# RMSNorm with Swish on one core: the first store in two pieces, and the next load behind it

## The chip, the cores and the metric

The kernel runs on one core of one Trainium2 chip. The core has five engines that run side by side and meet through semaphores: TensorE (PE, without work here), VectorE (DVE), ScalarE (ACT), GpSimd (POOL) and SyncE (SP), which here only issues transfers. 16 DMA engines move the data between the chip's main memory (HBM) and the on-chip buffer (SBUF, 128 partitions). The metric is the device time of one execution in microseconds (us). Beside the plain runs there is one profiled execution, from which all durations come.

## The reference

```python
batch, seq, dim = 16, 1024, 512          # x: float32, gamma: 512 ones, eps: 1e-5
rms = np.sqrt(np.mean(x ** 2, axis=-1, keepdims=True) + eps)
x_norm = x / rms * gamma
return x_norm * (1.0 / (1.0 + np.exp(-x_norm)))
```

16,384 rows of 512 float32 numbers go in and as many come out: 33.55 MB each way, 67.1 MB in all.

## The kernel before

**Tiling.** The 16,384 rows are dealt to the 128 partitions, 128 rows to each. In this document a "row" of the plan is one row on every partition, 128 x 2 KB = 256 KB. The 128 rows of the plan lie in four groups (32, 48, 16, 32); within a group a partition's rows are neighbours in HBM, so that a transfer of n rows is 128 runs of n x 2 KB. The SBUF buffer `xb` is a ring of 96 rows; results are written in place. Rows 96 to 127 of the plan take the places of rows 0 to 31, so loads 96, 112 and 122 may be issued only when the rows 0 to 31 have been stored.

**Transfers.** All of them are issued by SP, in the order of a list that is written out by hand (`order`), into one hardware queue. `loads` and `stores` give first row and number of rows; a transfer is named by its first row here (load 80 is rows 80 to 95). Entries of the list are:

- `("load", a)`: issue the load (line 115).
- `("store", a)`: issue the store when ACT has finished all units of 8 rows that it covers (line 121; the wait is part of the instruction, on `s_swish`).
- `("landed", a)`: SP waits until load a has landed (line 166).
- `("stored", 0)`: SP waits until store 0 has landed. In the trace this wait stands at the load behind it (line 115).

At the end SP waits for all the other stores, which share one semaphore (line 170). The first nine loads (rows 0 to 79) go out in the first 6 us, with gamma between them. Around the change the list says: when load 64 has landed, store 0 (32 rows), and load 80 directly behind it; when store 0 has landed, loads 96, 112 and 122; when load 112 has landed, all the other stores, each as soon as its rows are computed.

**Computation.** It goes in 16 units of 8 rows. For each unit ACT squares and sums six rows (line 215) and DVE two (line 251; in the first unit they do four each), POOL adds eps and takes the power -1/2 (lines 183, 189), DVE multiplies by that and by gamma (line 260), and ACT applies Silu in place, one instruction for 8 rows (line 225, for the last two units line 245). ACT and DVE run this as loops; PE's queue waits for the loads and passes each unit on to ACT.

Of the kernel before, what the change touches and what calls it, by code (L numbers as in the profile page):

```python
# [9 lines left out]
def kernel(  # L10
# [7 lines left out]
    nc = tc.nc  # L18
# [10 lines left out]
    ring = 96  # L29
    loads = [(0, 4), (4, 4), (8, 8), (16, 8), (24, 8), (32, 16), (48, 16), (64, 11), (75, 5)]  # L30
    loads += [(80, 16), (96, 16), (112, 10), (122, 6)]
    stores = [(0, 32), (32, 32), (64, 16), (80, 16), (96, 24), (120, 8)]
    order = [("load", a) for a in (0, 4, 8)] + [("gamma", 0)]
    order += [("load", a) for a in (16, 24, 32, 48, 64, 75)]
    order += [("landed", 64), ("store", 0), ("load", 80)]
    order += [("stored", 0), ("load", 96), ("load", 112), ("load", 122)]
    order += [("landed", 112)] + [("store", a) for a in (32, 64, 80, 96, 120)]
    early = 2
    cn = 8
# [15 lines left out]
    store_at = {a: t for t, (a, _) in enumerate(stores)}  # L55
# [21 lines left out]
    junk_v = [sbuf(f"junk_v{j}", [P, D]) for j in range(own_first)]  # L77

    ld = [nc.alloc_semaphore(f"ld{t}") for t in range(len(loads))]
    st = [nc.alloc_semaphore(f"st{t}") for t in range(2)]  # L80
    s_gld = nc.alloc_semaphore("s_gld")
    s_zero = nc.alloc_semaphore("s_zero")
    s_half = nc.alloc_semaphore("s_half")
# [10 lines left out]
    def need(ins, sem, value):  # L94
        return ins.wait_op(sem, value, "sem-ge")
# [4 lines left out]
    def dram(ap, piece):  # L100
        a, n = piece
        g = max(g for g in range(len(groups)) if first[g] <= a)
        r = a - first[g]
        assert r + n <= groups[g], piece
        rows = ap[P * first[g] : P * (first[g] + groups[g])]
        return rows.rearrange("(p n) d -> p n d", n=groups[g])[:, r : r + n, :]

    def buf(piece):
        a, n = piece
        at = a % ring  # L110
        assert at + n <= ring, piece
        return xb[:, at : at + n, :]

    def load(t):
        return nc.sync.dma_start(
            out=buf(loads[t]), in_=dram(xf, loads[t])
        ).then_inc(ld[t], 16)

    def store(t):
        need(  # L120
            nc.sync.dma_start(out=dram(of, stores[t]), in_=buf(stores[t])),
            s_swish, ends[t],
        ).then_inc(st[min(t, 1)], 16)

    def check_order():
        issued, stored = [], set()
# [26 lines left out]
    for what, a in order[early:]:  # L153
        if what == "load":
            load(load_at[a])
        elif what == "store":
            store(store_at[a])
        elif what == "gamma":
            need(
                nc.sync.dma_start(  # L160
                    out=gamma4[0:P:32, :], in_=gamma.partition_broadcast(4)
                ),
                s_zero, 1,
            ).then_inc(s_gld, 16)
        elif what == "landed":
            nc.sync.wait_ge(ld[load_at[a]], 16)
        else:
            assert store_at[a] == 0
            nc.sync.wait_ge(st[0], 16)
    nc.sync.wait_ge(st[1], 16 * (len(stores) - 1))  # L170

    for k in range(1, K):
        for t, (a, n) in enumerate(loads):
# [152 lines left out]
```

## Time and profile before

| What | us |
|---|---|
| median of three runs | 159.87 |
| lowest and highest | 159.64, 160.97 |
| the profiled execution | 161.05 |
| its span, first to last instruction | 159.7 |
| store 0: issued, landed | 48.12, 70.94 |
| load 80: issued, landed | 48.51, 81.0 |
| loads 96, 112, 122: issued | 70.96 to 71.8 |
| store 32 and store 64: issued | 96.89, 97.27 |
| store 80, 96, 120: issued | 110.02, 131.31, 136.61 |

The page gives the busy time of each engine, the DMA engines' load in 40 equal slices of the span, and groups of instructions by line. A name such as `SPq L115` means SP's instruction queue at line 115 of the kernel. In a row of the timeline the first number is the start, the second the duration, and what stands in brackets is the idle time of the engine before it and what ended that. In a row of a waits view the numbers are the total, the count and the longest. In a row of a windows view they are the window, its length, the busy time of DVE, ACT and POOL with the number of instructions, the clock, the mean share of the 16 DMA engines that was busy, and GB/s; a DMA packet is put down to the window in which it starts, so in windows that are shorter than a packet (2.4 us for 64 KB) the share can be above 1 or far below it without a pause.

### The profile page before, as it was taken

What the parts mean: (1) busy time and instruction counts of PE and PEld (TensorE: products, weight loads), DVE (VectorE), ACT (ScalarE), POOL (GpSimd) and SP (SyncE); (2) the same over time, 40 slices, a digit from 0 to 9 for tenths busy, and PEclk for the clock granted to TensorE, in tenths of its full rate; (3) what the DMA queues carried; (4) which work ended last, traced back from release to release, by engine and by line L of the source; (5) the groups of instructions that cost most, each with busy time, mean ns of one, the idle gap of its engine ahead of it and who ended that gap; (6) DMA issues with size and microseconds to landing.
All of it is one profiled execution on the core that took longest, in us unless ns stands there. A gap on an engine that the chain in (4) does not pass through costs nothing. (4 is left out here: it accounts for less than half of the span.)

```text
span 159.7 us, 844 instructions
## 1 busy us (share of the span) xinstructions
DVE 107.7 (67%) x198; ACT 115.8 (72%) x205; POOL 42.9 (27%) x38
## 2 busy tenths in 40 slices
DVE  0151999798988989898906988989898992000000
ACT  3609389999999999999269999999999186200000
POOL 1040506062442606062403351606153300000000
DMA  7999999999899969969999999799699999999993
GB/s 267 451 412 447 415 505 394 394 525 394 384 421 509 525 263 525 525 254 402 501 410 394 447 404 579 318 476 525 279 493 402 402 460 451 488 431 406 394 390 148
DMA packets 2744, 67.12 MB, mean 420 GB/s; under 512 B 308, under 2 KB 308, under 8 KB 312
## 3 DMA queue, kind: packets, MB, share of 16 engines
q1 hardware_dynamic: 2744, 67.12, 98.1%
HBM read 33.56 MB, written 33.55 MB: 420 GB/s over the span
## 5 line engine op out<-in xcount | busy, mean ns | idle before, releaser
L260 DVE SCALAR_TENSOR_TENSOR xb<-xb,rstd,gamma_sb 128x512 f32 (+1 forms) x128 | 86.1, 747 | 0.0
L215 ACT ACTIVATE junk<-xb 128x512 f32 (+1 forms) x94 | 54.6, 580 | 13.3 <-ACTq L98 11.7
L225 ACT ACTIVATE xb<-xb x14 | 50.4, 3603 | 0.7 <-ACTq L98 0.7
L251 DVE SCALAR_TENSOR_TENSOR junk_v<-xb 128x512 f32 (+1 forms) x34 | 22.1, 690 | 23.0 <-DVEq L98 23.0
L189 POOL TENSOR_TENSOR rstd<-aeps,neg_half 128x8 f32<-128x8 f32 x16 | 31.7, 1984 | 1.3
L183 POOL TENSOR_SCALAR aeps<-ms 128x8 f32<-128x8 f32 x16 | 10.3, 647 | 79.3 <-DVE junk_v L251 79.3
L215 ACT ACTIVATION_READ_ACCUMULATOR junk<-xb 128x1 f32 x94 | 17.7, 188 | 0.0
L245 ACT ACTIVATE xb<-xb 128x4096 f32<-128x4096 f32 x2 | 7.2, 3616 | 5.0 <-DVE xb L260 5.0
L251 DVE DVE_READ_ACCUMULATOR junk_v<-xb 128x1 f32 x34 | 2.8, 83 | 0.0
L227 ACT ACT_TABLE_LOAD x1 | 1.3, 1283 | 1.9 <-PEq L62 1.9
L269 DVE LOAD_MASK_SELECT gamma_sb<-gamma x1 | 0.0, 14 | 2.2 <-DMA gamma<-in_gamma_dram 2.2
L178 POOL MEMSET gamma<- 128x512 f32 x1 | 0.5, 525 | 1.5 <-POOLq L62 1.5
L269 DVE STREAM_SHUFFLE gamma_sb<-gamma 128x512 f32<-128x512 f32 x1 | 0.7, 719 | 0.0
L307 POOL MEMSET const-float32-0.0<- 128x1 f32 x1 | 0.1, 98 | 0.2 <-issue 0.2
L179 POOL MEMSET neg_half<- 128x8 f32 x1 | 0.1, 105 | 0.0
L307 POOL MEMSET const-uint8-127<- 128x1 uint8 x1 | 0.1, 102 | 0.0
L307 POOL MEMSET const-bfloat16-1.0<- 128x1 bf16 x1 | 0.1, 101 | 0.0
L307 POOL MEMSET const-float32-1.0<- 128x1 f32 x1 | 0.1, 98 | 0.0
## 6 DMA issues: line engine op xcount, KB each, us to landing
xb<-in_x_dram SPq DMA_DIRECT2D x4, 4096.0 KB, 30.0
out_dram<-xb SPq DMA_DIRECT2D x2, 4096.0 KB, 31.8
xb<-in_x_dram SPq DMA_DIRECT2D x3, 2048.0 KB, 13.8
out_dram<-xb SPq DMA_DIRECT2D x1, 6144.0 KB, 23.5
xb<-in_x_dram SPq DMA_DIRECT2D x1, 2816.0 KB, 43.0
xb<-in_x_dram SPq DMA_DIRECT2D x1, 2560.0 KB, 25.5
xb<-in_x_dram SPq DMA_DIRECT2D x2, 1024.0 KB, 5.7
out_dram<-xb SPq DMA_DIRECT2D x1, 2048.0 KB, 23.0
```

The lines of the kernel that those rows point to most:

```text
L178: nc.gpsimd.memset(gamma4, 0.0).then_inc(s_zero, 1)
L179: nc.gpsimd.memset(neg_half, -0.5).then_inc(s_half, 1)
L183: nc.gpsimd.tensor_scalar(out=aeps[k % 2], in0=ms[min(k, 1)], scalar1=eps_f, scalar2=None, op0=ALU.add,),
L189: nc.gpsimd.tensor_tensor(out=rstd[:, k * cn : (k + 1) * cn], in0=aeps[k % 2], in1=neg_half, op=ALU.pow),
L215: nc.scalar.activation(out=dummies[j], in_=rows[j], func=AF.Square, scale=inv_d**0.5, accum_out=sums[:, j : j + 1],)
L225: nc.scalar.activation(out=rows, in_=rows, func=AF.Silu).then_inc(s_swish, 1)
L227: nc.scalar.preload_act_table_set("silu_and_others")
L245: nc.scalar.activation(out=rows, in_=rows, func=AF.Silu), s_norm, n + 1
L251: ins = nc.vector.scalar_tensor_tensor(out=junk_v[j], in0=rows[j], scalar=inv_d, in1=rows[j], op0=ALU.mult, op1=ALU.mult, accum_out=to[:, ...
L260: ins = nc.vector.scalar_tensor_tensor(out=rows[j], in0=rows[j], scalar=factors[j], in1=gamma_sb, op0=ALU.mult, op1=ALU.mult,)
L269: need(nc.vector.stream_shuffle(gamma_sb, gamma4, [0] * 32), s_gld, 16).then_inc(s_gamma, 1)
L307: nc = _bacc.Bacc("TRN2", target_bir_lowering=False, num_devices=1)
```

## The change

Store 0 is cut into a store of 30 rows and one of 2, issued one behind the other. Load 80 is no longer issued together with the store: SP first waits until the 30 rows have landed, then issues load 80. Then it waits until the 2 rows have landed and issues loads 96, 112 and 122. Each of the two stores has a semaphore of its own; the other stores share the third.

```diff
-    stores = [(0, 32), (32, 32), (64, 16), (80, 16), (96, 24), (120, 8)]
+    stores = [(0, 30), (30, 2), (32, 32), (64, 16), (80, 16), (96, 24), (120, 8)]
...
-    order += [("landed", 64), ("store", 0), ("load", 80)]
-    order += [("stored", 0), ("load", 96), ("load", 112), ("load", 122)]
+    order += [("landed", 64), ("store", 0), ("store", 30)]
+    order += [("stored", 0), ("load", 80), ("stored", 30), ("load", 96), ("load", 112), ("load", 122)]
...
-    st = [nc.alloc_semaphore(f"st{t}") for t in range(2)]
+    st = [nc.alloc_semaphore(f"st{t}") for t in range(3)]
...
-        ).then_inc(st[min(t, 1)], 16)
+        ).then_inc(st[min(t, 2)], 16)
...
         else:
-            assert store_at[a] == 0
-            nc.sync.wait_ge(st[0], 16)
-    nc.sync.wait_ge(st[1], 16 * (len(stores) - 1))
+            nc.sync.wait_ge(st[store_at[a]], 16)
+    nc.sync.wait_ge(st[2], 16 * (len(stores) - 2))
```

Both stores wait for the same number of finished units (four), since row 30 and row 31 belong to the fourth unit. What is computed, and the bytes that are moved, stay the same.

## The prediction

> **What bounds the kernel now.** I read the page first, its busy shares and its row of the DMA engines:
>
> ```profile
> span 159.7 us, 844 instructions
> DVE 107.7 (67%) x198; ACT 115.8 (72%) x205; POOL 42.9 (27%) x38
> ...
> DMA  7999999999899969969999999799699999999993
> ...
> q1 hardware_dynamic: 2744, 67.12, 98.1%
> ```
>
> No compute engine is busy for three quarters of the span; the 16 DMA engines are, for 98.1% of it. A microsecond in which they idle is therefore a microsecond of kernel time, and everything else is cover. (A packet counts in the slice where it starts, so a 6 is no hole: in the trace's own table of packets no engine rests over 31 ns between two packets, from its first to its last.) The second view is busy time by windows, at the start, in the steady part and at the end; the last columns are DMA share and GB/s:
>
> ```profile
> 0.00:1.00 1.00, 0.00 (x0) 0.00 (x0) 0.19 (x4) 1.00 0.00 0
> 1.00:2.00 1.00, 0.00 (x0) 0.08 (x1) 0.09 (x1) 1.00 0.88 197
> 2.00:3.00 1.00, 0.00 (x0) 1.00 (x1) 0.48 (x2) 1.00 1.00 426
> ...
> 4.00:48.00 44.00, 32.89 (x66) 35.20 (x72) 14.39 (x12) 1.00 1.01 431
> ...
> 157.00:158.00 1.00, 0.00 (x0) 0.00 (x0) 0.00 (x0) 1.00 0.08 33
> 158.00:159.00 1.00, 0.00 (x0) 0.00 (x0) 0.00 (x0) 1.00 0.08 33
> ```
>
> Three things matter here. An issue into an empty queue moves nothing for 1 us. The steady rate is 431 GB/s: one row of the plan (128 x 2 KB = 262,144 B) takes 0.608 us. And after 157 us about one DMA engine of 16 still works: one engine is late, and it alone sets the last 1.5 us. The third view is SyncE's (SP's) timeline around the change, then what the waits of SP and ACT were worth:
>
> ```profile
> 48.12 0.35 SPq L121 DMA_DIRECT2D out_dram<-xb  x1
> 48.51 0.43 SPq L115 DMA_DIRECT2D xb<-in_x_dram  x1
> ```
> ```profile
> 70.96 1.29 SPq L115 DMA_DIRECT2D xb<-in_x_dram  x3
> ```
> ```profile
> SPq L115 <- DMA out_dram<-xb: 22.0, 1, 22.0
> ```
> ```profile
> 81.16 0.60 ACT L215 ACTIVATE junk<-xb 128x512 f32 x1 [4.33 <-ACTq L98]
> ```
>
> SP issues store 0 at 48.12 and load 80 right behind it, waits 22.0 us for store 0 to land, and issues loads 96, 112 and 122 at 70.96. All that time load 80 lies in the queue, so no DMA engine runs out. Issue-to-landing times of single transfers, from the same trace: store 0 22.8 us (landed 70.94), load 80 32.5 us (landed 81.0), load 0 at time zero 4.70 us.
>
> **The change, part by part.**
>
> *The split.* Same bytes, one more DMA. SP pays one more issue at 48.5, 0.33 to 0.43 us by the rows above; it is hidden by load 75, which is in the queue until it lands at 51.1 (issued 5.53, landing 45.6 us later). Per engine 8 packets of 64 KB (2.42 us each) become 8 of 60 KB and 8 of 4 KB. 8 KB packets take 0.309 us where the 64 KB rate gives 0.303, so eight more packets cost about 8 x 0.007 = 0.05 us; and this falls in a stretch that ends with a wait anyway. I take 0.
>
> *The moved load 80.* Its issue goes from 48.51 to the landing of the 30 rows. What is then queued is only the 2-row store, 2 x 0.608 = 1.21 us. Against it stands the loop "last byte moved, landing seen, next DMA issued, stream at full rate". The trace has one transfer into an empty queue: load 0, 4 rows, 4.70 us from issue to landing, of which 4 x 0.608 = 2.43 us is data. The rest, 2.27 us, holds the same pieces: issue and start 1.4 to 1.8 us (by packets, engine by engine), landing 0.45 us behind the last packet. Landing to SP's next issue: 0.02 us (70.94 to 70.96). The hole is 2.27 + 0.02 - 1.21 = 1.08 us on the engine that lands last.
>
> *What goes with it.* Today's turn from store to load isn't free either. Load 80 lands 10.06 us after store 0, its 16 rows are worth 9.73: 0.33 us. The packet table shows where: all 16 engines' last packets of store 0 are stretched, by 0.06 to 0.63 us, while load 80 stands behind them. In a hole of 1.08 us this turn is swallowed: 1.08 - 0.33 = 0.75 us. Bounds: with 0.45 us of landing, the 1.01 us to the first packet and nothing for a slow first packet, 0.45 + 0.02 + 1.01 - 1.21 = 0.27 us, less the turn about 0; with the longest landing of store 0 (0.67 us), the slowest start (1.77 us) and no turn saved, 0.67 + 0.02 + 1.77 - 1.21 = 1.25 us. I take **0.7 us**, near the full sum, since load 0 is the only row of a start on an empty queue.
>
> *The two waits.* Behind the first on SP stand load 80, the second wait, loads 96, 112, 122 and all later stores. The 2 rows land some 1.2 us behind the 30; the three loads then go out at about 70.5 to 71, as today (70.96), with 9.7 us of load 80 before them: cost 0. ACT feels load 80: today it idles 4.33 us until 81.16 for it, and would idle 0.7 us more, with VectorE and GpSimd behind it. That is hidden at the end: the 24-row store is issued at 131.31 when its Silu is done, while the store before it lands at 140.3 at last and at 138.0 on the first engine, 6.7 us ahead; it needs 2.27. Queue and computation shift together, so this cover of over 4 us stays. Without it the 0.7 us would not count twice either, as both are late by the same amount.
>
> **The sum.** The profiled execution took 161.05 us, 159.7 of span and 1.35 around it; plus 0.7 is a span of 160.4 and 161.75 us. That execution stands 1.2 us above the median of the runs, 159.87 (159.64 to 160.97); its late engine may be that difference. The step is the same for both: **160.6 us**.
>
> **The Trainium skill, two rules.** Both are in its page "DMA: Bandwidth & Descriptors", section "Latency and other measured facts". It gives about 0.6 us to the first byte for a DMA issued by SyncE or ScalarE. By it the loop would be an estimated 0.45 + 0.02 + 0.6 = 1.07 us, below the 1.21 us of the two rows, and there would be no hole. The trace disagrees: the first packet starts 1.01 us after issue, at time zero. It also gives 0.2 us for an access to HBM, and 2 us under high load, which it calls the main part of a DMA's fixed cost; by that, with 2 us of landing for 0.45, the estimated hole is 2.3 us after the turn. The store's 0.67 us under full load speaks against it.
>
> **The rivals.**
>
> *Covered.* A warm queue starts at once, the two rows last as long as the loop, and the bound of about 0 above holds: 159.9. For it: time zero is a cold start, its first packets took 0.4 to 0.8 us over their 0.309. Against: nothing in this trace shows a start that is shorter. The rule on the first byte would give this. Chance 0.17.
>
> *Slower by the late engine.* Today one engine loses 0.63 us in its last packet of store 0 and 0.51 in its first of load 80, 1.13 in all, and another 1.19 at the turn from load 122 to store 32 (98.3 to 100.3). If that is what a turn costs a weak engine, and the median run is free of it, a queue that starts anew into draining writes could bring it out each time, on top of the hole: 0.7 + 1.13 = 1.8, 161.7 us. It decides from 0.9 us of extra lateness on the engine that lands last. Against: the hole lets the writes drain first. Chance 0.15.
>
> *Slower by a long landing.* The 30 rows' completion takes 2 us instead of 0.45, as the rule on HBM under load has it: 0.7 + 1.5 = 2.2, 162.1 us. All store landings in the trace are 0.33 to 0.67 us behind the last packet. Chance 0.05.
>
> *The late engine set right.* Its 1.13 us at the turn vanish in the hole, and with separate turns the second lateness too: 0.7 - 1.13 - 1.19 = -1.6, 158.3 us. Both have to go. Chance 0.05.
>
> That the change doesn't do what it says I give nothing: in the compiled order load 80 stands behind both stores and waits for the first's semaphore, load 96 for the second's.
>
> **How the numbers follow.** The forecast, a hole of 0.2 to 1.25 us after the turn and so 160.0 to 161.2, has 0.58. With covered (from 159.5, where the runs' own spread lies) and the late engine (to 161.9) it makes 0.90: range 159.5 to 161.9. One per cent, 1.6 us, is about what a measurement of this kernel can tell from no change, as its three runs lie 1.33 us apart. Slower by more: the two slow rivals and a little of the forecast's upper end, 0.22. Faster by more: most of the last rival, 0.04. The rest, 0.74, is within 1%.
>
> **What would show it.** On SP: two stores at 48.1 and 48.5, one load at 69.2 to 69.7, three at 70.5 to 71. In the window 69 to 72 a real hole in the DMA's packets, about 1 us on each engine, that is not there today; load 80 landing at 81.2 to 81.8 and ACT's wait before unit 10 growing by the same amount; the rest of the run shifted by that, with no second hole. The start term is wrong if load 80's first packet comes less than 1 us, or over 1.8 us, after its issue. The landing term is wrong if SP issues load 80 after 70.2. The forecast is wrong as a whole if the hole is there and the end doesn't move, which would put the late engine, not the queue, in charge of the time.

## The result, and the profile after

The changed kernel takes 161.11 us in the median (161.03 to 161.39, six runs), the kernel before 159.80 (159.64 to 160.97, six runs beside them): a ratio of 1.006, with a 95% interval of 1.0031 to 1.009. In a second set of runs the same two gave 161.51 and 159.68, ratio 1.0098 (1.008 to 1.0116). So the change costs 0.6 to 1.0%, between 1.0 and 1.6 us by the ratios; the medians themselves lie 1.3 and 1.8 us apart. The forecast was 160.6 us, 0.7 over before, in a range of 159.5 to 161.9: right in sign and range, and low by 0.3 to 0.9 us in the cost (by the medians, 0.6 to 1.1).

The page of the kernel after, in the same rows:

```profile
span 159.8 us, 845 instructions
...
DVE 107.7 (67%) x198; ACT 115.7 (72%) x205; POOL 42.8 (27%) x38
...
DMA  7999999999999996979999999979969999999996
```

The span is 159.8 against 159.7 us, which seems to say that nothing happened. The reason is the profiled execution of the kernel before, which had the late DMA engine; a second profile of it, below, has a span of 158.1. In the mean of the 16 engines the last store landed 1.5 us later, at 159.20 us against 157.72. Busy times are unchanged, as they have to be. SP's timeline of the kernel after shows the new order, and behind it the time from issue to landing of load 80 alone (the transfer issued at 69.32):

```profile
48.12 0.82 SPq L121 DMA_DIRECT2D out_dram<-xb  x2
69.32 2.61 SPq L115 DMA_DIRECT2D xb<-in_x_dram  x4
```
```profile
DMA to landing us min/median/max: 12.3/12.3/12.3
```

Load 80 goes out at 69.32, when the 30 rows have landed, and lands at 81.6. Its 16 rows are 9.73 us of data, so some 2.5 us are fixed. The windows view around this issue:

```profile
68.50:70.05 1.55, 1.55 (x3) 1.55 (x3) 1.55 (x1) 1.00 0.79 322
70.05:70.41 0.36, 0.36 (x2) 0.36 (x3) 0.36 (x1) 1.00 0.00 0
70.41:70.95 0.54, 0.54 (x2) 0.54 (x3) 0.00 (x1) 1.00 3.28 971
```

In the middle window no packet starts, and by the trace's packet table none is running: the last packet of the two rows ends at 70.05, the first of load 80 starts at 70.42, 1.10 us after its issue. Engine by engine the pause is 0.38 to 1.35 us; from 66 to 74 us the engines idle 0.79 us each in the mean, where those of the kernel before idle nowhere. The rest is as it was: loads 96, 112 and 122 go out from 70.55 on, and no other pause follows. ACT's wait for load 80 has grown by 0.6 us:

```profile
81.75 0.60 ACT L214 ACTIVATE junk<-xb 128x512 f32 x1 [4.96 <-ACTq L98]
```

### The profile page after: what moved, and what is told of

Same layout as the page of the kernel before. It is cut to its first block, busy times and chain, and to the rows that moved or that the text cites. A ratio compares the mean times of both kernels' runs of the same rounds, so it can differ in the third digit from the quotient of the medians.

```text
span 159.8 us, 845 instructions
## 1 busy us (share of the span) xinstructions
DVE 107.7 (67%) x198; ACT 115.7 (72%) x205; POOL 42.8 (27%) x38
```

## The experiments

The theory is the hole: SP waits for a landing before it issues, and while landing, issue and start take their time, only the rows queued behind the awaited store keep the DMA engines busy. Rivals: the split costs by itself; any start of loads behind drained stores costs the same, however long the pause; the late engine decides. "Stretch" below is worked out from the packet table: what packets take beyond the median packet of their size, summed over a window and divided by 16 engines. "The turn" is the passage of the full queue from one direction to the other, from stores to loads or back.

### The split alone

```diff
-    order += [("landed", 64), ("store", 0), ("store", 30)]
-    order += [("stored", 0), ("load", 80), ("stored", 30), ("load", 96), ("load", 112), ("load", 122)]
+    order += [("landed", 64), ("store", 0), ("store", 30), ("load", 80)]
+    order += [("stored", 0), ("stored", 30), ("load", 96), ("load", 112), ("load", 122)]
```

> The first store stays in two pieces of 30 and 2 rows, but load 80 is issued together with them again, so the queue never runs short. Hole theory (the cost is the time in which the queue is empty): as before, 159.8 us, within 0.2. Split theory (the two pieces cost by themselves): about 161, as the changed kernel. The profile should show no pause of the DMA engines near 70 us.

Measured: 160.43 us against 159.97 before, ratio 1.0019 (1.0 to 1.0037). No engine pauses from 66 to 74 us. The split is thus not the main cost, though it is over the 0.2 us that were expected at most: 0.3 us by the ratio, 0.46 by the medians. The stretch from 66 to 73 us, the turn from store to load, is about 0.6 us an engine here (0.56 or 0.65, by the median 4 KB packet of this kernel or of the changed one), and 0.27 in the kernel before (0.19 in its second profile). All of it lies in the 4 KB packets ahead of the turn; load 80's packets take their median. In the changed kernel it is the other way round: the 4 KB packets take their median, and the stretch of 0.58 us lies in load 80's packets. So the split's dear turn is no part of what the changed kernel loses.

### The wait alone

```diff
-    order += [("landed", 64), ("store", 0), ("load", 80)]
-    order += [("stored", 0), ("load", 96), ("load", 112), ("load", 122)]
+    order += [("landed", 64), ("store", 0)]
+    order += [("stored", 0), ("load", 80), ("load", 96), ("load", 112), ("load", 122)]
```

> The first store is whole again (32 rows), but load 80 waits for its landing, so that nothing is queued behind the store. Hole theory: 2.27 us from the fixed part of load 0's landing, plus 0.02, less the turn of 0.33 us that goes with it: 2.0 us over before, 161.8; with the 0.4 us by which the changed kernel exceeded its forecast, 162.2. Turn theory (what costs is that loads start anew behind drained stores, however long the pause): as the changed kernel, 161.1.

Measured: 162.32 us against 159.97, ratio 1.0139 (1.0116 to 1.0163), 2.2 us. Idle 2.07 us an engine. The windows view of this kernel, from the end of its store on:

```profile
69.50:71.50 2.00, 2.00 (x4) 2.00 (x7) 1.15 (x1) 1.00 0.00 0
71.50:73.50 2.00, 1.60 (x3) 2.00 (x9) 0.00 (x0) 1.00 0.96 279
```

For 2 us no packet starts. The store's last packets end between 69.67 and 70.15, SP issues load 80 at 70.62, and its first packet starts at 71.58. This is the wait's price without cover, and it falls with the hole theory, not with the theory that the price doesn't depend on the pause.

### The cover, row by row

The second store with 1, 3, 4 and 8 rows in place of 2; the first has the rest of 32. The edit for 4 rows, the others likewise:

```diff
-    stores = [(0, 30), (30, 2), (32, 32), (64, 16), (80, 16), (96, 24), (120, 8)]
+    stores = [(0, 28), (28, 4), (32, 32), (64, 16), (80, 16), (96, 24), (120, 8)]
...
-    order += [("landed", 64), ("store", 0), ("store", 30)]
-    order += [("stored", 0), ("load", 80), ("stored", 30), ("load", 96), ("load", 112), ("load", 122)]
+    order += [("landed", 64), ("store", 0), ("store", 28)]
+    order += [("stored", 0), ("load", 80), ("stored", 28), ("load", 96), ("load", 112), ("load", 122)]
```

> Pieces of 31 and 1 rows, load 80 issued when the 31 have landed. 1 row covers 0.61 us. Hole theory: half way between whole store (2.2 us over before) and 2 rows (1.0 to 1.6), so 1.6 to 1.9 over before, 161.4 to 161.7 us. A theory of thresholds: 161.1, as with 2 rows.

> Pieces of 29 and 3 rows, load 80 issued when the 29 have landed. 3 rows cover 1.82 us. Hole theory: between 2 rows (1.0 to 1.6 us over before) and 4 rows (0.1): one row less of cover is 0.61 us, so 0.4 to 0.9 over before, 160.2 to 160.6 us. A theory of thresholds (any drained write costs the same) would put it at 161.1 or at 159.8.

> Pieces of 28 and 4 rows, load 80 issued when the 28 have landed. Hole theory: 4 rows are 2.43 us of cover, the loop takes 2.29, so the hole is closed: 159.8 us, at most 0.3 over before. Turn theory: the same 161.1 as with 2 rows.

> Pieces of 24 and 8 rows, load 80 issued when the 24 have landed. Hole theory: 8 rows are 4.86 us of cover, no hole: 159.8 us, as before. Turn theory: 161.1. If it is clearly below before, a late issue of load 80 has a gain of its own, up to the 0.33 us of the turn.

| Rows queued behind | Median, before beside it | Ratio (95%) | Idle an engine, 66 to 74 us | Stretch an engine, 66 to 73 us |
|---|---|---|---|---|
| 0 | 162.32, 159.97 | 1.0139 (1.0116 to 1.0163) | 2.07 | 0.64 |
| 1 | 161.61, 159.88 | 1.0102 (1.0073 to 1.013) | 1.11 | 0.72 |
| 2 | 161.11, 159.80 | 1.006 (1.0031 to 1.009) | 0.79 | 0.58 |
| 2, again | 161.51, 159.68 | 1.0098 (1.008 to 1.0116) | 0.82 | 0.66 |
| 3 | 160.47, 159.88 | 1.0048 (1.0028 to 1.0068) | 0.17 | 0.68 |
| 4 | 160.20, 159.97 | 1.0007 (0.9989 to 1.0026) | 0 | 0.58 |
| 8 | 160.14, 159.97 | 1.0006 (0.9981 to 1.0032) | 0 | 0.22 |

The price falls with each row; with four and with eight rows it can't be told from nothing. The stretch does not follow the rows: from 0 to 4 rows it is 0.58 to 0.72 us and lies in load 80's packets, also where no engine pauses; only with 8 rows is it as in the kernel before (0.27 and 0.19), and lies in the store's last packets again. Load 80's time from issue to landing, with 0, 1 and 3 rows behind the store, one row from each kernel's answer in this order:

```profile
DMA to landing us min/median/max: 12.4/12.4/12.4
```
```profile
DMA to landing us min/median/max: 12.2/12.2/12.2
```
```profile
DMA to landing us min/median/max: 12.5/12.5/12.5
```

Less 9.73 us of data this is a fixed part of 2.5 to 2.8 us, where load 0 at time zero has 2.27. With 2.7 us in place of 2.27, chosen afterwards from these, and a turn of 0.25 us that is paid anyway, a hole of 2.7 - 0.608 n - 0.25 gives 2.4, 1.8, 1.2, 0.6 and 0 us for 0 to 4 rows. The packet table needs no such choice: idle time and stretch, less the 0.23 us of stretch before (mean of two profiles), are 2.5, 1.6, 1.1 and 1.2, 0.6, 0.3 and for 8 rows 0. Measured, by the ratios: 2.2, 1.6, 1.0 to 1.6, 0.8, 0.1 and for 8 rows 0.1. None of these versions is faster than the kernel before; 4 or 8 rows only bring it back.

### Both kernels again, for a second trace

> The kernel before once more, for a second trace. If one DMA engine's lateness is chance, the span comes out near 158.4 us instead of 159.7, with the engines' last packets less than 1.5 us apart, and the time near 159.8. If it belongs to the kernel, one engine is again about 1.5 us behind the rest after 157 us.

> The changed kernel once more. Besides its time (161.1 us), its trace answers whether the second loss comes again: the first profile had packets of load 122 stretched at 98 to 100 us, 0.4 us an engine against 0.1 in the kernel before. Theory H (the hole only, and the stretch is chance): the stretch is absent or of another size, the time stays at 161.1. Theory H+T (the pause leads to a costlier turn at load 122): 0.3 to 0.5 us again.

The second profile of the kernel before, its page's first row and one window at the end, and then the kernel after in the same stretch:

```profile
span 158.1 us, 844 instructions
...
157.00:158.00 1.00, 0.00 (x0) 0.00 (x0) 0.00 (x0) 1.00 0.01 0
```
```profile
157.00:158.00 1.00, 0.00 (x0) 0.00 (x0) 0.00 (x0) 1.00 0.99 426
158.00:159.00 1.00, 0.00 (x0) 0.00 (x0) 0.00 (x0) 1.00 0.69 295
```

The late engine is gone: from 157 us on, when the first profile of the same program had one engine at work (share 0.08 in each of two windows), nothing is left. That execution took 159.43 us. So not every execution of the kernel before has a late engine, and the two first profiles could not be compared at their ends. In this pair the 16 engines of the kernel after are at work for another 1.7 us in the mean, so the time is lost by all, not by one.

Where it is lost, by landings (last engine) in this second pair: load 80 lands at 81.64 against 80.12, 1.5 us later; load 96 at 91.32 against 89.83, 1.5; load 122 at 102.19 against 99.87, 2.3. A second loss of some 0.4 us or more thus seems to come at load 122. The stretch from 97 to 103 us shows it as well: 0.44 and 0.50 us an engine in the two profiles of the kernel after, 0.09 and 0.15 in those before. It was expected to vanish if it were chance; it came again.

### The second loss

```diff
-    order += [("landed", 112)] + [("store", a) for a in (32, 64, 80, 96, 120)]
+    order += [("landed", 96)] + [("store", a) for a in (32, 64, 80, 96, 120)]
```

> The changed kernel, with the later stores released by the landing of load 96 instead of load 112, so that store 32 is issued some 6 us earlier, near 91.3 us, with 16 rows in the queue before it instead of 6. If the stretched packets at 98 to 100 us come from the issue itself, they move to 91 to 94 us; if they come from the turn from loads to stores, they stay at 98 to 100 us, and the time stays at 161.1; if they come from a queue that is nearly short there, they vanish and the time falls by 0.3 to 0.4 us.

> The same edit on the kernel before: store 32 issued near 90.7 us. If the turn at 98 to 100 us costs it its late engine because the store comes late, the time falls by up to 0.3 us and its spread (159.64 to 160.97) narrows; otherwise 159.8, as before.

On the changed kernel: 161.36 us, ratio to the kernel before 1.01 (1.0082 to 1.0118); store 32 is issued at 91.19, and the stretch from 96 to 106 us is 0.85 us, at the old place. So neither the issue itself nor a queue that is nearly short makes it; it goes with the turn from loads to stores. On the kernel before: 159.86 us, 1.0019 (0.9996 to 1.0041), and the spread didn't narrow (159.53 to 161.46).

Then the two last loads as one, so that the turn is made by 32 KB packets:

```diff
-    loads += [(80, 16), (96, 16), (112, 10), (122, 6)]
+    loads += [(80, 16), (96, 16), (112, 16)]
...
-    order += [("stored", 0), ("load", 80), ("stored", 30), ("load", 96), ("load", 112), ("load", 122)]
-    order += [("landed", 112)] + [("store", a) for a in (32, 64, 80, 96, 120)]
+    order += [("stored", 0), ("load", 80), ("stored", 30), ("load", 96), ("load", 112)]
+    order += [("landed", 96)] + [("store", a) for a in (32, 64, 80, 96, 120)]
```

> The changed kernel with loads 112 and 122 joined into one load of 16 rows, and the later stores released by the landing of load 96, so that the turn from loads to stores at 98 to 100 us is made by packets of 32 KB in place of 12 KB. If the stretch of 0.4 to 0.5 us an engine is a matter of the small packets at that turn, it goes, and the time is 160.7 to 160.9 us; if every such turn behind a pause is stretched, it stays, near 161.3.

> The same edit on the kernel before, as the partner of the run above. The hole alone should then be their difference: 1.1 to 1.3 us (1.08 reckoned from load 0, less the turn of 0.2 to 0.3, plus first packets that are slower). 159.4 to 159.8 us, without a clear difference from the kernel before.

Changed kernel: 161.62 us, 1.0098 (1.0073 to 1.0123), stretch from 96 to 106 us 0.97 us. Kernel before: 160.28 us, 1.0031 (1.0003 to 1.0058), stretch 0.93, so the expectation of "no difference" was missed for this one. Between the two medians lie 1.3 us, between the ratios 1.1; 1.1 to 1.3 were expected of the hole.

The small packets are not the cause: with larger ones the stretch doesn't fall. But the early store alone raises it, in both kernels alike: 0.85 and 0.84 us with store 32 issued early, 0.97 and 0.93 with the two last loads joined as well, where the changed kernel had 0.44 and 0.50 and the kernel before 0.09 and 0.15. (The turn of the kernel before begins at 96.4 us in these two versions, so a window from 97 us on misses a third of its stretch.) So with the early store the changed kernel has no more of it than its partner, and the extra 0.35 us are seen only with the store in its old place.

What a stretch here costs in time isn't shown: with 0.4 us more of it the changed kernel with the early store took 161.36 us, between its two medians of 161.11 and 161.51. And the partners' profiles in these last two pairs, 161.46 and 161.29 us, had a late engine and lie 1.6 and 1.0 us above the medians of their kernels, so they can't fix what the turn costs there. Nor does the stretch simply follow the pause: with 0 to 8 rows of cover it was 0.30, 0.51, 0.44 to 0.50, 0.04, 0.24 and 0.04. Why the turn is dearer in the changed kernel stays open.

## Why the prediction was right, and where it was off

**The bound.** Right. The DMA engines are full; the versions that made them pause became slower, the more the longer the pause, and those without a pause stayed within 0.5 us of the kernel before.

**The split, taken as 0.** With load 80 issued early it measured 1.0019, 0.3 us with an interval from 0 to 0.6. My argument, 8 more packets at 7 ns, looked at the packets' own time and not at the turn behind them, which went from 0.19 and 0.27 us to about 0.6. For the changed kernel the 0 was right all the same: its 4 KB packets, with nothing queued behind them, take their median.

**The hole.** The mechanism is shown: the pause is in the packets, its size falls with each row of cover, and it closes at 4 rows, where 2.43 us of cover outlast landing, issue and the first packet's start. What doesn't close there is the slow start: 0.58 us of stretch in load 80's packets, gone with 8 rows. To this extent the rival holds by which any start behind drained stores costs the same. The times of these two versions (1.0007 and 1.0006) don't tell them apart. The dates were right: load 80 issued at 69.32 (69.2 to 69.7 forecast), the first of the three loads at 70.55 (about 70.5 to 71), the first packet 1.10 us after its issue (1 to 1.8), load 80 landed at 81.59 (81.2 to 81.8).

**The size.** This is the step that was off, mostly by one term, the loop: 2.27 us taken from load 0 at time zero; 2.5 to 2.8 measured. With the changed kernel's own 2.54 us the sum is 2.54 + 0.02 - 1.21 = 1.35 us in place of 1.08, and the packets say the same: 0.79 us idle and 0.58 us of stretch in load 80's packets. I had asked whether a warm queue would start faster than the cold one; it starts no faster (0.96 to 1.10 us to the first packet against 1.01), and 15 of the 16 engines' first packets of load 80 are stretched by 0.3 to 1.1 us against their median, as at time zero. The idle time alone is three times the 0.27 us of my lower bound, since SP waits for the slowest of 16 engines and the engines start one after the other: their last packets of the 30 rows end between 68.34 and 68.79 us, and their first ones of load 80 start between 70.42 and 70.94. The second term is the turn that the hole swallows. It is saved, as forecast, since no store packet is stretched any more; but 0.33 us was the figure of one landing, on the engine that came last, and in the mean of the engines the turn is 0.27 us in that profile and 0.19 in the second. Both terms together make 1.1 to 1.3 us (0.79 + 0.58 - 0.27, and 0.82 + 0.66 - 0.19 in the second pair), where I had 0.75. My upper bound of 1.25 us was nearly the value, but by another sum, with no turn saved.

**No second loss.** "The rest shifted, with no second hole" holds for pauses. But there were 0.35 us more of stretched packets at the turn from loads to stores, which no step of mine had. With them the sum is 1.4 to 1.7 us, against 1.0 to 1.6 by the ratios and 1.3 and 1.8 by the medians. That they add to the time is argued, not shown: with 1 row of cover, where the turn from loads to stores is as dear (0.51 us), pause and slow start alone already make up the measured 1.6 us.

**The two waits and ACT.** Right: the three loads cost nothing, since load 80 lay in the queue. ACT waited longer for load 80, 4.96 us for 4.33, and 5.09 for 3.55 in the second pair, and the end didn't feel it: the 24-row store went out at 131.9 us, while the store before it landed at 139.6 on its first engine, 7.7 us ahead.

**The rivals.** "Covered" fell: the shortest start into an empty queue was 0.96 us (with the wait alone), so the Trainium skill's 0.6 us to the first byte ("DMA: Bandwidth & Descriptors", section "Latency and other measured facts") doesn't hold here as the time from SP's issue to a packet's start. Counted from the end of SP's issuing instruction, which itself takes 0.33 to 0.39 us, the first packet comes after 0.62 to 0.76 us, near that figure. The long landing fell too: the 30 rows landed 0.51 us behind their last packet, not 2 us, with all engines still at work. The late engine fell as a cause: it came in three of four profiles with load 80 behind an undivided store (before, not before again, and the two variants of before) and in neither of the kernel after. I had named it as what may set the profiled execution 1.2 us above the median; the second profile, 159.43 us without it, bears that out. The other side of that rival, the late engine set right, has something for it: the six first runs of the kernel after lie within 0.4 us of each other, those of the kernel before within 1.3. But in the second set both spread alike (0.8 and 0.9 us), and no run of the changed kernel was faster than the median before.

## What to carry to other kernels

Where the DMA queue is the bound and an issue waits for a landing, price the cover: issue to landing less the data's own time (here 2.5 to 2.8 us) must be covered by what is queued behind the awaited transfer; here 4 rows of 256 KB, about 1 MB, were enough for no pause and no measurable cost, and each row short of it cost about 0.6 us. Take that fixed part from a transfer into an empty queue in the same trace, and expect it to be somewhat longer in mid-kernel (2.27 there, 2.5 to 2.8 here). Take a turn that the pause swallows from the mean of all engines, not from the one that lands last. And before two profiles are compared at their end, look whether a single DMA engine sets one of them; a second profile of the same program costs little and would have settled it.

## What the runs showed of the hardware that was not expected

- One DMA engine of 16 ended 1.3 us behind the next in one execution and 0.1 us behind it in another of the same program: spans of 159.7 and 158.1 us.
- The turn from store packets to load packets, on a queue that never ran short, cost 0.19 to 0.28 us an engine behind 64 KB packets, 0.22 behind 16 KB and about 0.6 behind 4 KB ones, nearly all of it in the store packets. Where the load was issued so late that at most 4 rows were queued before it, the store packets took their median and the load's first packets were stretched instead, by 0.58 to 0.72 us an engine, whether the engines paused (2.07 us) or not.
- The turn from loads to stores cost 0.02 to 0.15 us an engine in the kernel before, with the split alone and with 3 or 8 rows of cover, and 0.24 with 4 rows; 0.44 and 0.50 in the changed kernel, 0.51 with 1 row and 0.30 with none. With the store issued 6 us earlier, and more rows queued before it, it was 0.84 to 0.97 us in both kernels, and neither became faster.
